# The last down-projection with stationary activations, and a final norm that is finished by half of the rows

## The chip, the cores and the metric

The kernel runs on one core of a Trainium2 chip. The metric is device time in microseconds (us), the median of the runs. Times inside the execution come from one profiled run of the kernel. PE is the matrix engine (TensorE; PEld is its loading of the stationary operand), DVE is VectorE, ACT is ScalarE, POOL is GpSimd, SP is SyncE, which here issues nearly all transfers.

## The reference, cut to what matters

256 tokens of width 2048 go through two layers with a residual stream `h`, and a last RMSNorm. Each layer has a token mixer (a gated MLP in the first, an attention in the second) and a ConvFFN. The end of the program, which the change touches, is the second layer's ConvFFN and the norm behind it:

```python
def rmsnorm(x, g):
    r = lax.rsqrt(jnp.mean(xf * xf, axis=-1, keepdims=True) + EPS)
    return (xf * r).astype(x.dtype) * g

def conv_ffn(xn, w_up, conv_w, conv_b, w_down):      # 2048 -> 2 x 5632 -> 5632 -> 2048
    h = xn @ w_up
    ...                                              # causal conv of width 3, gate, value
    return (jax.nn.silu(gate) * val) @ w_down

h = h + conv_ffn(rmsnorm(h, f_norm[l]), f_w_up[l], f_conv_w[l], f_conv_b[l], f_w_down[l])
...
return rmsnorm(h, final_norm)
```

## The kernel before, in words

**Products.** All weights are float32 and are streamed once from HBM in chunks of 128 x 1024 (512 KB). ACT rounds a chunk to fp32r (`whi`, L84) and DVE makes the remainder (`wlo`, L85); activations are kept as such a pair too (`X1`, `mlp_X2`, `att_X2`, `ffn_H`: columns 0 to 255 the rounded tokens, 256 to 511 the remainders). A product is then three matmuls: rounded by rounded, rounded by remainder, remainder by rounded. One chunk makes 24 matmuls with 256 moving columns each, and each has its own load of a stationary 128 x 128.

**Two roles.** In `feat_block` the weights are stationary and the 256 tokens are moving: the result is feature-major (features on partitions). In `tok_blocks` the activations are stationary, 128 tokens at a time, and the weights are moving: the result is token-major. Stages in the order of the program: `a_in_v` (tok), `a_in_u`, `a_out`, `up0`, `down0` (feat), `b_q` (tok), `kvf_f` (a small one), `kvf_k`, `kvf_v` (tok), `b_g`, `b_out`, `up1`, `down1` (feat). The weights of a `tok` stage lie 32 elements further into their tile than those of a `feat` stage (`FEAT_AT, TOK_AT = 0, 32`, L32).

**Order.** Nothing is scheduled by a tool: `Stream.run` (L88) walks the chunks in order, and for chunk i it issues the load of chunk i+6, the split of chunk i+3, and the products of chunk i; then it steps every pending generator once (`advance`), which is how evictions, norms and transposes are spread over later chunks. Loads wait on SP in this order.

**Wide products.** `between()` (L170) sets `state["wide"]` to `[8, 2]`: of the next chunk 8 matmuls, and of the one after it 2, are issued with 512 moving columns in place of two with 256. It is called where PE does something small between products (sums over tokens, transposes, attention heads), and once in every eleven blocks of `up` (L554).

**The end.** `h` is feature-major, `[128, 16, 256]`. Blocks p = 0 to 6 of `down1` add their result to `h`, square it into `acc` and multiply it with the last gain (`final`, L371). Block 7 goes through `last_tiles` and `last_tile`: its last chunk first finishes one 128-feature tile, then the other. `output` (L389) sums the squares over partitions with matmuls against ones, transposes all of `h` to token-major on PE (32 transposes, L399), computes the factor on ACT and DVE, scales eight 128 x 512 pieces out of PSUM (L420 and L422), and sends 2 MB out with five transfers on SP (L424, L426).

Of the kernel before, what the change touches and what calls it, by code (L numbers as in the profile page):

```python
# [17 lines left out]
P = 128  # L18
# [8 lines left out]
SCALE = 128 ** -0.5  # L27
AHEAD = 3
# [6 lines left out]
C_ANORM, C_KVNORM, C_BNORM, C_FNORM, C_FINAL, C_AVNORM = 0, 16, 32, 48, 80, 96  # L35
C_KNORM, C_QNORM, C_BF = 112, 113, 114
C_CONVW = 115
# [97 lines left out]
def build(ctx, tc, d, out):  # L135
# [8 lines left out]
    col = const.tile([P, C_ALL], F32, name="col")  # L144
    h = const.tile([P, KD, T], F32, name="h")
# [7 lines left out]
    small.tile([P, 56], F32, name="place")  # L153
# [24 lines left out]
    def feat_block(src, x, K, done, tiles=None):  # L178

# [5 lines left out]
        for c in range(n):  # L185
            def mult(hi, lo, c=c):
                if c == 0:
                    box["ps"], box["both"] = tiles[0]() if tiles else main_ps(), False
                ps, xx, wide = box["ps"], x(), wide_next()
                box["both"] |= wide > 0  # L190
                if not tiles:
                    ps = [ps[:, m, :] for m in range(2)]

                def rounded(j, m):
                    nonlocal wide
                    w = hi[:, j * 256 + m * P:j * 256 + (m + 1) * P]
                    kt = 4 * c + j
                    if wide > 0:
                        mm(ps[m], w, xx[:, kt, :], kt == 0, False)
                        wide -= 1  # L200
                    else:
                        for half in range(2):
                            mm(ps[m][:, :T], w, xx[:, kt, half * T:(half + 1) * T], kt == 0 and half == 0, False)

                def remainder(j, m):
                    kt = 4 * c + j
                    mm(ps[m][:, :T], lo[:, j * 256 + m * P:j * 256 + (m + 1) * P], xx[:, kt, :T],
                       False, kt == K - 1)

                if tiles and c == n - 1:  # L210
                    for m in range(2):
                        for j in range(4):
                            rounded(j, m)
                        for j in range(4):
                            remainder(j, m)
                        tiles[1](m, ps[m])
                else:
                    for product in (rounded, remainder):
                        for j in range(4):
                            for m in range(2):  # L220
                                product(j, m)
# [4 lines left out]
    def tok_block(src, x, done):  # L226
        tok_blocks([(src, done)], x)

    def tok_blocks(blocks, x, load=None, prep=None):
# [4 lines left out]
        cuts = [(c, 0, 2) for c in range(8)]  # L234
        if prep:
            cuts[:1] = [(0, 0, 1), (0, 1, 1)]
        for c, j0, nj in cuts:
            if prep and c == 3:
                s.then(at_mult=between)
            for i, ((src, done), box) in enumerate(zip(blocks, boxes)):  # L240
                def mult(hi, lo, c=c, j0=j0, nj=nj, done=done, box=box):
# [4 lines left out]
                    for j in range(nj):  # L246
                        kt = kt0 + j

                        def product(tb, lower, part):
# [3 lines left out]
                            for i in range(0, 512, n):  # L253
                                mm(ps[:, tb, i:i + n], xx[:, kt, at:at + P], part[:, j * 512 + i:j * 512 + i + n],
                                   kt == 0 and i == 0 and part is hi and not lower, kt == KD - 1 and lower == 1)
# [7 lines left out]
                    if kt0 + nj == KD:  # L263
                        s.start(done(ps))
# [86 lines left out]
    def last_tiles():  # L351

        tail["pairs"] = [main_ps() for _ in range(3)]
        tail["banks"] = [misc_ps() for _ in range(2)]
        return tail["pairs"][0][:, 0, :], tail["banks"][0]

    def last_tile(m, ps):

        kt = KD - 2 + m
        if m == 0:  # L360
            tail["sq"] = small.tile([P, 2, T], F32, name="sq", tag="sq", bufs=2)
        nc.vector.tensor_tensor(h[:, kt, :], h[:, kt, :], ps[:, :T], op=OP.add)
        nc.scalar.activation(tail["sq"][:, m, :], h[:, kt, :], AF.Square)
        nc.scalar.activation(h[:, kt, :], h[:, kt, :], AF.Copy, scale=column(C_FINAL + kt))

# [5 lines left out]
    def final(p, gain):  # L371

        def done(ps, both):
            if p == 7:
                output()
                return
            hh = h[:, 2 * p:2 * p + 2, :]
            nc.vector.tensor_tensor(hh, hh, ps[:, :, :T], op=OP.add)
            if both:
                nc.vector.tensor_tensor(hh, hh, ps[:, :, T:], op=OP.add)  # L380
            square_into_acc(p)
            for kt in (2 * p, 2 * p + 1):
                nc.scalar.activation(h[:, kt, :], h[:, kt, :], AF.Copy, scale=column(gain + kt))
            if p == 5:
                nc.scalar.activation(warm, ones, AF.Sqrt)
            yield
        return done

    def output():  # L389

        pairs, banks = tail["pairs"], tail["banks"]
        sums = banks[1]
        place = {(0, 0): pairs[1][:, 0, :], (1, 0): pairs[2][:, 0, :], (0, 1): pairs[1][:, 1, :],
                 (1, 1): pairs[2][:, 1, :], (0, 2): pairs[0][:, 0, :], (1, 2): pairs[0][:, 1, :],
                 (0, 3): banks[0], (1, 3): banks[1]}

        def transposes(tb, quad):
            for j in range(4):
                nc.tensor.transpose(place[tb, quad][:, j * P:(j + 1) * P],  # L399
                                    h[:, 4 * quad + j, tb * P:(tb + 1) * P], ident)  # L400

        sum_tokens(sums, acc, True, False)
        sum_tokens(sums, tail["sq"][:, 0, :], False, False)
        transposes(0, 0)
        sum_tokens(sums, tail["sq"][:, 1, :], False, True)
        t = small.tile([P, 2], F32, name="rs_t", tag="rs_t2", bufs=2)
        v = small.tile([P, 2], F32, name="ts_v", tag="ts_v", bufs=2)
        nc.vector.tensor_scalar(v, sums[:, :2], 1.0 / D, EPS, op0=OP.mult, op1=OP.add)
        nc.scalar.activation(t, v, AF.Sqrt)
        for quad in range(4):  # L410
            for tb in range(2):
                if tb or quad:
                    transposes(tb, quad)
        nc.vector.reciprocal(rcol, t)
        newton(rcol, v, t)
        for quad in range(4):
            o = h[:, 4 * quad:4 * quad + 4, :].rearrange("p a b -> p (a b)").rearrange("p (a b) -> p a b", a=2)
            for tb in range(2):
                if tb == 0:
                    nc.vector.tensor_scalar(o[:, tb, :], place[tb, quad], rcol[:, tb:tb + 1], None, op0=OP.mult)  # L420
                else:
                    nc.scalar.activation(o[:, tb, :], place[tb, quad], AF.Copy, scale=rcol[:, tb:tb + 1])  # L422
                if quad == 0:
                    nc.sync.dma_start(out[quad][:, tb, :], o[:, tb, :])  # L424
            if quad:
                nc.sync.dma_start(out[quad], o)  # L426
# [124 lines left out]
    def ffn(l, done):  # L551
# [4 lines left out]
        for p in range(8):  # L556
            feat_block(d[f"down{l}"][11 * p:11 * p + 11], ffn_h, KF, done(p), (last_tiles, last_tile) if l and p == 7 else None)
# [8 lines left out]
    def blocks_turned(src, n):  # L566


        turned = ph.temp("turned", [P, 512])[:, :n * P].rearrange("p (c h j) -> p c h j", c=4, h=n)
# [318 lines left out]
```

## Time and profile before

| | |
|---|---|
| median of 3 runs | 2194.79 us (2194.67 to 2195.84) |
| the profiled run's own time | 2194.7 us |
| its span, first to last instruction | 2193.0 us |
| PE busy | 2183.9 us of it, 18684 matmuls |
| DVE, ACT busy | 1455.7 us, 1140.6 us |
| DMA | 437.61 MB, mean 200 GB/s |
| granted TensorE clock | 0.999 |

So 1.7 us of the time lie outside the span. Matmuls are pipelined: one matmul of 256 columns is shown as 276 to 282 ns long, and the next starts long before its end, so the pace of PE is the distance between starts (or a count in a stretch of time), and not the length of a row. A row of the timeline merges equal instructions that follow each other; "x16" are 16 of them.

### The profile page before, as it was taken

The page shows a single profiled execution, that of the slowest core. Times are in us where ns is not written, and L with a number is a line of the kernel's source. Part 1 is how long each engine was busy: PE and PEld are TensorE (multiplying, and loading weights), DVE is VectorE, ACT ScalarE, POOL GpSimd, SP SyncE. Part 2 cuts the span into 40 slices and gives each one's busy share as a digit, 9 for nine tenths or more (in the row PEclk, how much of TensorE's full clock was granted, in tenths as well). Part 3 has the DMA queues.
Part 4 walks back from the last instruction along what each step waited for, and adds up shares of the span by engine and source line. Part 5 has one row for each costly group of instructions (what it writes and reads, how often), then busy time and mean ns, then how long its engine had stood idle before and what let it go on. Part 6 is the DMA issues. An engine that isn't in the chain of part 4 may idle for free.

```text
span 2193.0 us, 44738 instructions
## 1 busy us (share of the span) xinstructions
PE 2183.9 (100%) x18684; PEld 2158.3 (98%) x18684; DVE 1455.7 (66%) x2031; ACT 1140.6 (52%) x1517; POOL 19.0 (1%) x41
## 2 busy tenths in 40 slices
PE   9999999999999999999999999999999999999998
PEld 9999999999999999999999999999999999999998
DVE  6676677777777754556786776667777777764443
ACT  5644455555555544444544655455555555544443
POOL 0000000000000000000000100000000000000000
PEclk9999999999999999999999999999999999999999
DMA  8565566666666666666677776556666666666664
GB/s 307 179 188 177 197 197 195 187 202 189 197 194 195 196 184 203 193 196 205 218 226 255 233 227 196 183 197 196 195 195 195 194 193 190 198 197 194 193 194 134
DMA packets 139964, 437.61 MB, mean 200 GB/s; under 512 B 24032, under 2 KB 34672, under 8 KB 139504
## 3 DMA queue, kind: packets, MB, share of 16 engines
q1 hardware_dynamic: 138816, 432.62, 62.4%
q8 instruction: 146, 2.39, 0.5%
q0 software_dynamic: 768, 2.10, 0.4%
q14 instruction: 58, 0.48, 0.1%
q10 hardware_dynamic: 176, 0.02, 0.0%
HBM read 425.22 MB, written 9.45 MB: 198 GB/s over the span
## 4 chain that ended last, share of the span: by engine, by line
PE 99%; DMA 0%; DVE 0%; ACT 0%; ACTq 0%; issue 0%; SPq 0%; DVEq 0%
PE ps L168 97%; PE mp L168 1%; DMA raw<-a_in_v 0%; PE mp L508 0%; PE mp L761 0%; PE mp L760 0%; PE mp L756 0%; PE mp L755 0%; PE mp L754 0%; PE mp L368 0%; DVE h L420 0%; DVE wlo L85 0%; ACT whi L84 0%; ACTq L882 0%; PE mp L308 0%
## 5 line engine op out<-in xcount | busy, mean ns | idle before, releaser
L85 DVE TENSOR_TENSOR wlo<-raw,whi 128x1024 fp32r<-128x1024 f32 (+1 forms) x787 | 954.6, 1219 | 455.2 <-ACT whi L84 447.1
L84 ACT ACTIVATE whi<-raw 128x1024 fp32r<-128x1024 f32 (+1 forms) x787 | 827.3, 1056 | 720.4 <-PE ps L168 655.2
L168 PE MATMUL ps<-X,whi 128*128 128x256 f32 (+1 forms) x6406 | 825.6, 281 | 0.0
L168 PEld LDWEIGHTS ps<-X,whi 128*128 128x128 f32 x6406 | 772.5, 188 | 9.0
L168 PE MATMUL ps<-X,wlo 128*128 128x256 f32 x3328 | 445.4, 276 | 0.0
L168 PEld LDWEIGHTS ps<-X,wlo 128*128 128x128 f32 x3328 | 410.5, 188 | 2.3
L168 PE MATMUL ps<-ffn_H,whi 128*128 128x256 f32 x2728 | 342.7, 276 | 0.0
L168 PEld LDWEIGHTS ps<-ffn_H,whi 128*128 128x128 f32 x2728 | 324.5, 188 | 0.0
L168 PE MATMUL ps<-ffn_H,wlo 128*128 128x256 f32 x1364 | 186.6, 276 | 0.0
L168 PEld LDWEIGHTS ps<-ffn_H,wlo 128*128 128x128 f32 x1364 | 169.9, 188 | 0.0
L542 DVE SCALAR_TENSOR_TENSOR ffn_c<-ffn_a,col,ffn_c 128x255 f32<-128x255 f32 x352 | 162.0, 481 | 6.3
L168 PE MATMUL ps<-whi,att_X 128*128 128x256 f32 (+1 forms) x928 | 164.0, 292 | 0.0
L168 PE MATMUL ps<-whi,X 128*128 128x256 f32 (+1 forms) x989 | 159.1, 281 | 0.2 <-ACT whi L84 0.2
L168 PEld LDWEIGHTS ps<-whi,att_X 128*128 128x128 f32 x928 | 130.5, 188 | 6.2
L168 PEld LDWEIGHTS ps<-whi,X 128*128 128x128 f32 x989 | 133.4, 188 | 2.4 <-ACT whi L84 0.4
L334 DVE TENSOR_TENSOR ffn_a<-ps,rB 128x512 f32<-128x512 f32 x76 | 52.6, 692 | 115.2 <-PE ps L168 115.2
L538 ACT ACTIVATE ffn_c<-ffn_a,col 128x256 f32<-128x256 f32 x176 | 96.3, 594 | 48.8 <-DVE ffn_a L334 48.8
L168 PE MATMUL ps<-wlo,X 128*128 128x256 f32 (+1 forms) x491 | 99.4, 282 | 0.8 <-DVE wlo L85 0.8
L168 PE MATMUL ps<-wlo,att_X 128*128 128x256 f32 (+1 forms) x448 | 100.1, 293 | 0.0
L168 PEld LDWEIGHTS ps<-wlo,X 128*128 128x128 f32 x491 | 74.6, 188 | 1.5 <-DVE wlo L85 1.0
L274 ACT ACTIVATE X<-h,col 128x256 fp32r<-128x256 f32 x64 | 29.1, 501 | 82.4 <-DVE h L340 77.6
L168 PEld LDWEIGHTS ps<-wlo,att_X 128*128 128x128 f32 x448 | 69.9, 188 | 1.9
(157 smaller groups left out, 1133.4 us busy)
## 6 DMA issues: line engine op xcount, KB each, us to landing
raw<-up SPq DMA_DIRECT2D x352, 512.0 KB, 4.0
raw<-down SPq DMA_DIRECT2D x176, 512.0 KB, 3.9
raw<-a_in_u SPq DMA_DIRECT2D x32, 512.0 KB, 4.2
raw<-a_out SPq DMA_DIRECT2D x32, 512.0 KB, 4.3
raw<-b_q SPq DMA_DIRECT2D x32, 512.0 KB, 4.3
raw<-kvf_k SPq DMA_DIRECT2D x32, 512.0 KB, 4.6
raw<-kvf_v SPq DMA_DIRECT2D x32, 512.0 KB, 4.8
raw<-b_g SPq DMA_DIRECT2D x32, 512.0 KB, 4.3
```

The costliest lines, as they stand in the source:

```text
L84: self.nc.scalar.activation(hi[:, :n], raw, AF.Copy)
L85: self.nc.vector.tensor_tensor(lo[:, :n], raw, hi[:, :n].bitcast(F32), op=OP.subtract)
L168: nc.tensor.matmul(o, a, b, start=start, stop=stop, skip_group_check=True)
L274: nc.scalar.activation(dst[:, kt, :T], h[:, kt, :], AF.Copy, scale=g)
L334: nc.vector.tensor_tensor(a, src, rB[:, None, :].to_broadcast([P, 2, T]), op=OP.mult)
L538: nc.scalar.activation(c[:, m, :], a[:, m, :], AF.Identity, scale=w[2], bias=column(C_CONVB + l * 2 * KF + f))
L542: nc.vector.scalar_tensor_tensor(c[:, m, n:], a[:, m, :T - n], w[k], c[:, m, n:], op0=OP.mult, op1=OP.add)
```

## The change

`down1` becomes a `tok` stage. Its 2048 output columns are 3 blocks of 512 (`tok_block`, 22 chunks each), one of 256 (`short_block`, 11 chunks) and a last one of 256 (`last_block`, 11 chunks). All of its matmuls have 256 moving columns. In the last block the products of the second 128 tokens are held back for the last four chunks (`HELD = 4`): first the first 128 tokens are finished for all chunks and `output(0, ...)` is issued, then the 48 held matmuls, then `output(1, ...)`.

The residual stream has to be token-major for this. `residual_by_token`, started in the third block of `up1`, turns `h` in eight pieces: a DVE transpose of 32 x 32 blocks, four transfers to DRAM on SP, and later one transfer back on SP into the same memory. The columns come out in a permuted order, which the host's arrangement of `f_w_down[1]`, of the last gain and of the result follows. The last gain is loaded as a row, broadcast over partitions, on POOL. Sums of squares are taken by ACT as it squares (`accum_out`), so that the end has no sums and no transposes on PE. Two tiles that nothing uses (`spare`, and `place` made larger) keep the other tiles where they were, or move them by 512 bytes a partition in all.

The core of the diff:

```diff
-    small.tile([P, 56], F32, name="place")
+    small.tile([P, 152], F32, name="place")
...
-    def last_tiles():
...
-    def output():
...
+    def residual_by_token():
+        gains = ph.keep("gains", [P, D])
+        nc.gpsimd.dma_start(gains, d["final"].to_broadcast([P, D]))
+        ways = []
+        for tb in range(2):
+            for g in range(4):
+                turned = blocks_turned(h[:, 4 * g:4 * g + 4, tb * P:(tb + 1) * P])
+                yield
+                ways.append(rows_out(f"h{tb}{g}", turned))
+                yield
+        for tb in range(2):
+            for g in range(4):
+                yield
+                rows_in(by_token()[:, tb, g * 512:(g + 1) * 512].rearrange("p (r x) -> p r x", r=4), ways.pop(0))
+
+    def add_block(tb, cols, ps, into):
+        hh = by_token()[:, tb, cols]
+        sq = small.tile([P, 2, T], F32, name="sq", tag="sq", bufs=2).rearrange("p a b -> p (a b)")
+        nc.vector.tensor_tensor(hh, hh, ps, op=OP.add)
+        nc.scalar.activation(sq[:, :ps.shape[1]], hh, AF.Square, accum_out=into)
...
+    def short_products(ps, c, tb, x, K, hi, lo):
+        for j in range(4):
+            kt = 4 * c + j
+            for lower, part in ((0, hi), (0, lo), (1, hi)):
+                at = lower * T + tb * P
+                mm(ps, x()[:, kt, at:at + P], part[:, j * T:(j + 1) * T],
+                   kt == 0 and part is hi and not lower, kt == K - 1 and lower == 1)
+
+    def last_block(src, x, K):
+        n, held, ps = K // 4, [], []
+        for c in range(n):
+            def mult(hi, lo, c=c):
+                if c == 0:
+                    ps.extend(main_ps()[:, 0, :T] for _ in range(2))
+                if c < n - HELD:
+                    for tb in range(2):
+                        short_products(ps[tb], c, tb, x, K, hi, lo)
+                    return
+                held.append((c, hi, lo))
+                short_products(ps[0], c, 0, x, K, hi, lo)
+                if c == n - 1:
+                    output(0, ps[0])
+                    for cc, h2, l2 in held:
+                        short_products(ps[1], cc, 1, x, K, h2, l2)
+                    output(1, ps[1])
+            s.chunk(src[c], mult, TOK_AT)
+
+    def output(tb, ps):
...
+        add_block(tb, last, ps, ss)
+        nc.scalar.activation(t, ss, AF.Sqrt, scale=1.0 / D, bias=v)
+        nc.vector.tensor_tensor(hg, o[:, last], gains[:, last], op=OP.mult)
+        nc.vector.scalar_tensor_tensor(nv, ss, -0.5 / D, nv, op0=OP.mult, op1=OP.add)
+        nc.vector.reciprocal(y, t)
+        nc.vector.tensor_scalar(t, y, y, nv, op0=OP.mult, op1=OP.mult)
+        nc.vector.scalar_tensor_tensor(r, t, 1.5, y, op0=OP.add, op1=OP.mult)
+        nc.scalar.activation(o[:, :512], o[:, :512], AF.Copy, scale=r)
+        nc.scalar.dma_start(out[tb][:, :512], o[:, :512])
+        nc.vector.tensor_scalar(o[:, last], hg, r, None, op0=OP.mult)
+        nc.vector.tensor_scalar(o[:, 1536:1792], o[:, 1536:1792], r, None, op0=OP.mult)
+        nc.sync.dma_start(out[tb][:, 1536:], o[:, 1536:])
+        for blk in (1, 2):
+            cols = slice(blk * 512, (blk + 1) * 512)
+            nc.vector.tensor_scalar(o[:, cols], o[:, cols], r, None, op0=OP.mult)
+            nc.sync.dma_start(out[tb][:, cols], o[:, cols])
...
-    ffn(1, lambda p: final(p, C_FINAL))
+    ffn_up(1)
+    for blk in range(3):
+        tok_block(d["down1"][22 * blk:22 * blk + 22], ffn_h, final(blk), KF)
+    short_block(d["down1s"][:11], ffn_h, KF, final(3))
+    last_block(d["down1s"][11:], ffn_h, KF)
```

How the instructions move, at the two places that the prediction speaks of. The first is PE where `up1` ends and `down1` begins; `X_73` (`X_74` after the change) is `X1`, and "ps<-A,B" has the moving operand A ahead of the stationary B. Before:

```order
L168 MATMUL ps<-X_73,whi 128x256 x16
L168 MATMUL ps<-X_73,wlo 128x256 x8
L168 MATMUL ps<-ffn_H,whi 128x256 x16
L168 MATMUL ps<-ffn_H,wlo 128x256 x8
L168 MATMUL ps<-ffn_H,whi 128x256 x16
L168 MATMUL ps<-ffn_H,wlo 128x256 x8
```

And with the change:

```order
L170 MATMUL ps<-X_74,whi 128x256 x16
L170 MATMUL ps<-X_74,wlo 128x256 x8
L170 MATMUL ps<-whi,ffn_H 128x256 x2
L170 MATMUL ps<-wlo,ffn_H 128x256 x2
L170 MATMUL ps<-whi,ffn_H 128x256 x4
L170 MATMUL ps<-wlo,ffn_H 128x256 x2
L170 MATMUL ps<-whi,ffn_H 128x256 x4
```

The operands change places between two matmuls of 256 columns, and no wide product or other work of PE stands there or anywhere behind it. The second place is the end of the program on DVE. Before:

```order
L362 TENSOR_TENSOR h<-h,ps 128x256
L362 TENSOR_TENSOR h<-h,mp 128x256
L408 TENSOR_SCALAR ts_v<-mp 128x2
L414 RECIPROCAL rcol<-rs_t 128x2
L290 SCALAR_TENSOR_TENSOR rs_t<-rcol 128x2
L291 TENSOR_TENSOR rs_t<-rs_t,ts_v 128x2
L292 SCALAR_TENSOR_TENSOR rcol<-rs_t,rcol 128x2
L420 TENSOR_SCALAR h<-ps,rcol 128x512 x3
L420 TENSOR_SCALAR h<-mp,rcol 128x512
```

With the change these rows stand there for each half of the tokens (here the second half's):

```order
L372 TENSOR_TENSOR h<-h,ps 128x256
L447 TENSOR_TENSOR ffn_hg<-h,ffn_gains 128x256
L448 SCALAR_TENSOR_TENSOR ffn_nv<-ffn_ss,ffn_nv 128x1
L449 RECIPROCAL fin_y<-fin_t 128x1
L450 TENSOR_SCALAR fin_t<-fin_y,ffn_nv 128x1
L451 SCALAR_TENSOR_TENSOR rcol<-fin_t,fin_y 128x1
L454 TENSOR_SCALAR h<-ffn_hg,rcol 128x256
L455 TENSOR_SCALAR h<-h,rcol 128x256
L459 TENSOR_SCALAR h<-h,rcol 128x512 x2
```

The sums that DVE took from PE (L408) are gone, and half as much is scaled behind the last matmul, from SBUF.

More of the change, by code (lines that the diff above doesn't have):

```diff
@@ L187, in mult @@
                 if c == 0:
-                    box["ps"], box["both"] = tiles[0]() if tiles else main_ps(), False
+                    box["ps"], box["both"] = main_ps(), False
                 ps, xx, wide = box["ps"], x(), wide_next()
                 box["both"] |= wide > 0
-                if not tiles:
-                    ps = [ps[:, m, :] for m in range(2)]
                 def rounded(j, m):
@@ L202, in rounded @@
                         for half in range(2):
-                            mm(ps[m][:, :T], w, xx[:, kt, half * T:(half + 1) * T], kt == 0 and half == 0, False)
+                            mm(ps[:, m, :T], w, xx[:, kt, half * T:(half + 1) * T], kt == 0 and half == 0, False)
                 def remainder(j, m):
                     kt = 4 * c + j
-                    mm(ps[m][:, :T], lo[:, j * 256 + m * P:j * 256 + (m + 1) * P], xx[:, kt, :T],
+                    mm(ps[:, m, :T], lo[:, j * 256 + m * P:j * 256 + (m + 1) * P], xx[:, kt, :T],
                        False, kt == K - 1)
[L210 to L221, printed above, removed]
+                for product in (rounded, remainder):
+                    for j in range(4):
+                        for m in range(2):
+                            product(j, m)
                 if c == n - 1:
@@ L254, in product @@
                                 mm(ps[:, tb, i:i + n], xx[:, kt, at:at + P], part[:, j * 512 + i:j * 512 + i + n],
[L255 removed]
+                                   kt == 0 and i == 0 and part is hi and not lower, kt == K - 1 and lower == 1)
                         if nj == 1:
@@ L369, in sum_tokens, with by_token @@
                              start=first and tb == 0, stop=last and tb == 1, skip_group_check=True)
[L371 to L384, printed above, removed]
+    def by_token():
+        return h.rearrange("p a b -> p (a b)").rearrange("p (t f) -> p t f", t=2)
@@ L385, in done @@
                 nc.scalar.activation(warm, ones, AF.Sqrt)
-            yield
         return done
-    def output():
[L391 to L426, printed above, removed]
@@ L555, in ffn @@
                 s.then(at_mult=between)
-        for p in range(8):
-            feat_block(d[f"down{l}"][11 * p:11 * p + 11], ffn_h, KF, done(p), (last_tiles, last_tile) if l and p == 7 else None)
+            if l and i == 2:
+                s.then(at_mult=lambda: s.start(residual_by_token()))
     def att(key):
@@ L809, in build @@
         feat_block(d["a_out"][4 * p:4 * p + 4], mlp_x2, KD, residual(p, C_FNORM))
-    ffn(0, lambda p: residual(p, C_BNORM))
+    ffn_up(0)
+    for p in range(8):
+        feat_block(d["down0"][11 * p:11 * p + 11], ffn_h, KF, residual(p, C_BNORM))
     s.then(at_mult=lambda: s.start(kv_operand()))
```

111 lines of the change are left out of this document (73 added, 38 removed).

## The prediction

> **What bounds the kernel now.** I read the page's first part and the chain of waits, then the end of the timeline, then PE's pace stage by stage.
>
> ```profile
> PE   9999999999999999999999999999999999999998
> PE 99%; DMA 0%; DVE 0%; ACT 0%; ACTq 0%; issue 0%; SPq 0%; DVEq 0%
> ```
>
> PE is never idle, and the chain that ends last is PE for 99%. So two things alone can move the time: the number of matmuls times their pace, and what follows the last matmul. The number does not change: `down1` is 2112 matmuls (88 chunks of 24) in both kernels. The end, first from the chain (start, length):
>
> ```profile
> 2180.25 1.36 PE mp L168 x12
> 2181.61 0.78 PE mp L368 x8
> ```
>
> From the timeline of DVE and ACT, in order of time:
>
> ```profile
> 2181.65 0.42 DVE L362 TENSOR_TENSOR h<-h,mp 128x256 f32<-128x256 f32 x1 [0.94 <-PE mp L168]
> 2182.11 0.42 ACT L363 ACTIVATE sq<-h 128x256 f32<-128x256 f32 x1 [0.40 <-DVE h L362]
> 2183.47 0.20 ACT L409 ACTIVATE rs_t<-ts_v 128x2 f32<-128x2 f32 x1 [0.40 <-DVE ts_v L408]
> 2183.70 0.17 DVE L414 RECIPROCAL rcol<-rs_t 128x2 f32<-128x2 f32 x1 [0.27 <-ACT rs_t L409]
> 2183.90 0.16 DVE L290 SCALAR_TENSOR_TENSOR rs_t<-rcol 128x2 f32<-128x2 f32 x1
> 2184.29 0.16 DVE L292 SCALAR_TENSOR_TENSOR rcol<-rs_t,rcol 128x2 f32<-128x2 f32 x1
> 2184.56 2.07 DVE L420 TENSOR_SCALAR h<-ps,rcol 128x512 f32<-128x512 f32 x3
> ```
>
> And the five output transfers by line, with one microsecond of the table of windows while they run (its last number is GB/s):
>
> ```profile
> L424 SPq DMA_DIRECT2D out<-h x2: 343/384/425, 2185.3 to 2185.7; - x2
> DMA to landing us min/median/max: 2.0/2.2/2.3
> L426 SPq DMA_DIRECT2D out<-h x3: 332/408/412, 2186.3 to 2188.0; - x3
> DMA to landing us min/median/max: 3.1/3.3/4.0
> 2188.00:2189.00 1.00, 0.00 (x0) 0.00 (x0) 0.00 (x0) 0.00 (x0) 0.00 (x0) 1.00 1.01 397
> ```
>
> The last product ends at E = 2181.61 us and the span at 2193.0: 11.4 us. The factor is ready at E + 2.84 (2184.29 + 0.16), the last transfer is issued at 2188.0 and lands 4.0 later, at 2192.0, and 1.0 us of closing work follows. The 2 MB leave at about 400 GB/s. So the end is a chain of small steps and then a transfer.
>
> **PE's pace.** The table of windows gives it: behind the stretch and its length stand PE's busy time and its count, then the same of PEld, DVE, ACT and POOL (where PE was asked for alone, only PE), and the granted clock. Matmuls that each show as 0.28 us touch a stretch W in number N with (W + 0.28) / pace = N.
>
> ```profile
> 1028.00:1068.00 40.00, 40.00 (x355) 1.00 0.77 249
> 2020.00:2100.00 80.00, 80.00 (x708) 1.00 0.60 188
> 97.00:108.00 11.00, 11.00 (x96) 11.00 (x95) 8.79 (x18) 6.14 (x8) 0.00 (x0) 1.00 0.38 125
> 1118.00:1130.00 12.00, 12.00 (x108) 12.00 (x107) 11.66 (x23) 5.18 (x5) 0.00 (x0) 1.00 0.66 186
> ```
>
> The first is `b_q`, with activations stationary as the change wants them: 40.28 / 355 = 113.5 ns. The second is `down1` as it is: 80.28 / 708 = 113.4 ns. Steady, the two roles cost the same. The third is the beginning of `a_in_u`: 11.28 / 96 = 117.5 ns, 4% slower at full clock. The fourth, in `kvf_k`, is fast (113.7) with DVE busy for 11.66 of 12 us, so a busy DVE is not the reason. Where does the slow pace begin and end?
>
> ```profile
> 94.89 0.39 PE L168 MATMUL ps<-whi,X 128*128 128x256 f32 x2
> 95.12 2.04 PE L168 MATMUL ps<-X,whi 128*128 128x256 f32 x16
> ...
> 108.31 1.11 PE L168 MATMUL ps<-X,wlo 128*128 128x256 f32 x8
> 109.25 1.06 PE L508 MATMUL mp<-mlp_wT,mlp_vt 128*128 128x128 f32 x8
> ...
> 995.84 1.07 PE L168 MATMUL ps<-ffn_H,wlo 128*128 128x256 f32 x8
> 996.75 0.40 PE L168 MATMUL ps<-whi,X 128*128 128x256 f32 x2
> ...
> 1002.17 0.40 PE L168 MATMUL ps<-whi,X 128*128 128x256 f32 x2
> 1002.41 0.50 PE L368 MATMUL mp<-ones,acc 128*128 128x1 f32 x4
> ```
>
> Both times it begins at the matmul where the operands change places: from 995.84 to 996.75 stand 8 matmuls at 113.8 ns, from 996.75 to 1002.17 46 (two chunks less two) at 117.8. From 95.12 to 108.31 (112 matmuls) it is 117.8 too. And both times it lasts until PE does something else, the small matmuls at 109.25 and 1002.41 with the wide products that `between` puts behind them. Later the same operands run fast (`b_q` above). It looks like a state that an exchange of roles sets and an interruption clears, not like a property of a role.
>
> **The change part by part.** (1) *Pace.* The exchange from `up1` to the new `down1` is the one at 996.75 again: weights stationary before, activations stationary behind, and the tiles' addresses in the built programs are the same but for 512 bytes in `H`. What cleared the state there is missing: `down1` has no sums, no heads, no wide product. If the state is set and lasts, 2112 matmuls pay 117.8 - 113.4 = 4.4 ns: +9.3 us (4.1 to 4.5 ns by the other quotients: 8.7 to 9.5). If it is not set: 0.
>
> The Trainium skill, page "TensorE: Matmul & The Clock Gate", section "Step-by-step: what each phase is for", says that the two operands come through independent read ports, so that loading the next weights takes nothing from the running matmul. By it the exchange could not matter and this term would be 0; the rows at 95.12 and 996.75 disagree with it in their two stretches.
>
> (2) *The end.* Sums on PE, transposes, four of the eight scalings and 1 MB of transfers leave the stretch behind the last matmul. What stays is priced by the rows above and these (behind the bar: busy us, mean ns):
>
> ```profile
> L483 ACT ACTIVATION_READ_ACCUMULATOR sq<-mlp_vt 128x1 f32 x8 | 1.5, 186 | 0.0
> L633 ACT ACTIVATE att_q<-att_rows,att_gain 128x512 f32<-128x512 f32 x8 | 5.7, 712 | 0.0
> L725 DVE TENSOR_SCALAR att_big<-att_big,att_sm 128x256 f32<-128x256 f32 x16 | 5.6, 348 | 0.0
> L493 DVE TENSOR_SCALAR mlp_vt<-mlp_vt,mlp_rv 128x2048 f32<-128x2048 f32 x2 | 2.5, 1286 | 0.0
> L570 DVE STREAM_TRANSPOSE att_turned<-att_big 128x512 f32<-128x512 f32 x16 | 11.4, 712 | 0.6
> ```
>
> Add to E + 0.46, square to E + 0.92, reading the accumulator (0.19) to E + 1.11, square root to E + 1.33, reciprocal to E + 1.53, two small steps 0.2 apart: the factor at E + 1.93. DVE starts 0.11 later (as 2184.45 to 2184.56), scales 256 columns twice (0.35 each) and 512 twice (0.48 each, an estimate on the line between the rows of 256 and 2048 columns): E + 3.7. ACT's 512 columns (0.71) end before that, at E + 2.8. So the first transfer goes out at E + 2.8, the last at E + 3.8. A transfer of 256 KB took 2.0 to 2.3: E + 6.0; 1 MB at 400 GB/s is 2.6 us behind a start of about 0.9 us (the 2.2 of a 256 KB transfer less its 0.65 of data, rounded down): E + 6.3. I take 6.3, since the four overlap. With 1.0 us of closing work the span ends at E + 7.3 instead of E + 11.4: -4.1 us. Bounds: with the worst landing of the large ones (4.0) E + 8.8 and -2.6; with DVE's pieces at 0.35 each and landings of 2.0, E + 6.5 and -4.9.
>
> The first half must be out of the way: it starts 48 matmuls (5.7 us) earlier, its last scaling ends 3.7 us after that, and its transfers by E + 0.6; the second half wants DVE at E and the queues at E + 2.8. If it were late, at most its 1 MB, 2.6 us, would stand in the way.
>
> (3) *Turning the residual.* 8 transposes of 0.71 us on DVE over 16 chunks of `up1`, 32 small and 8 large transfers on SP, one load on POOL, where nothing stands behind it. What hides it:
>
> ```profile
> 1470.00:1650.00 180.00, 180.00 (x1555) 178.57 (x1554) 132.00 (x186) 101.86 (x138) 0.00 (x0) 1.00 0.63 196
> SPq L578 <- DVE att_turned L570: 3.2, 4, 1.4
> ```
>
> DVE is busy 132 of 180 us in this stage; 5.7 us more in 16 chunks (43.5 us) raise 0.73 to 0.86. On SP the loads of weights stand behind transfers that wait for a transpose: in `b_q`, which does the same exchange eight times, such a wait was 1.4 us at most, and PE's pace there is the 113.5 above. Loads are issued three chunks (8.2 us) ahead of their split. Cost 0; if this cover failed, eight waits of 1.4 us would reach PE: +11 us.
>
> (4) The split of weights, the number and size of the loads, and the evictions' size per chunk stay: 0, under PE as now.
>
> **Sum**, against the profiled span: 2193.0 + 9.3 - 4.1 = 2198.2; with the 1.7 us outside it 2199.9 us. The profiled run (2194.7) lies 0.1 below the median of 2194.79, so the sum can stand beside the median.
>
> **Rivals.** *The fast pace holds* (chance 0.24): the state is not set here, or is left at once. For it: two cases are few, and both lie where a norm changes the work of ACT and DVE as well, which is not so here. Against it: both begin at the very matmul, and keep one pace while the other engines' work goes on changing. Then only the end counts: 2193.0 - 4.1 + 1.7 = 2190.6 us, not slower. By the Trainium skill's rule above this is the case to expect.
>
> *The state is shed on the way* (0.10), for instance where the first block ends, after 528 matmuls (2.3 us): 2192.9 us. For it speaks nothing seen; against it that the stretch at 95.12 passed four edges of chunks, one of them of a block (24 matmuls a chunk, 4 chunks a block), and stayed slow.
>
> *The exchange of the residual starves PE* (0.03): +11 us from (3), 2201.6 with a fast `down1` and 2210.9 with a slow one. Against it speaks `b_q`.
>
> **How the numbers follow.** Slow to the end has 0.63 and gives 2199.9; its own range, 8.7 to 9.5 and -2.6 to -4.9, is 2198.5 to 2201.6. The fast case (2189.8 to 2192.1) holds 0.24, too much to leave out: the range is 2190.0 to 2201.6. What a measurement of this kernel can tell from no change is about 0.2%, 4.4 us: the bounds are 2190.4 and 2199.2. Slower: four fifths of 0.63, and the starved case: 0.53. Faster: half of the fast case: 0.13. The rest, 0.34, is no change that can be told.
>
> **What would show it.** In the profile after, a stretch of 80 us in `down1` would hold about 682 matmuls where 708 were, from the first block on to the last; the last matmul would end about 9 us after 2181.61, and the span 7.3 us behind it. Wrong would be: 708 in 80 us (the first rival); a count that jumps within the stage (the second); idle PE in `up1` (the third); an end of 8.8 us or more; or a slow pace that is there in `up1` already, which would make the exchange of roles the wrong cause.

## The result, and the profile after

| | before | after |
|---|---|---|
| median | 2195.19 us (8 runs, 2194.31 to 2195.9) | 2201.5 us (8 runs, 2200.94 to 2202.2) |
| span of the profiled run | 2193.0 us | 2199.6 us |
| first matmul of `down1` starts | 1942.09 us | 1942.31 us |
| last product of weights ends | 2181.61 us | 2191.21 us |
| from there to the end of the span | 11.4 us | 8.4 us |

The changed kernel takes 1.0029 times the time of the kernel before (95% interval 1.0019 to 1.0038): 0.3% slower, 6.3 us between the medians and 6.6 us between the spans. The products of `down1` take 9.4 us more, the end behind them 3.0 us less, and the stage starts 0.2 us later: 9.4 - 3.0 + 0.2 = 6.6. The 0.2 us were there long before the changed stages: `a_in_u` begins at 95.43 us where it began at 95.12.

The chain that ended last, by engine, is still PE for 99%:

```profile
PE 99%; DMA 0%; DVE 0%; ACT 0%; issue 0%; SPq 0%; DVEq 0%; ACTq 0%
```

The table of windows of the changed kernel, PE alone (stretch, length, busy time and count, granted clock, share of the DMA engines, GB/s). Two stretches lie in `down1`:

```profile
2020.00:2100.00 80.00, 80.00 (x681) 1.00 0.61 189
2100.00:2180.00 80.00, 80.00 (x682) 1.00 0.56 173
```

Where 708 matmuls stood in 80 us there are 681 and 682, at a clock of 1.00 and with PE never idle: 80.28 / 681.5 = 117.8 ns each. The stretch in `up1` in which the residual is turned, all engines:

```profile
1470.00:1650.00 180.00, 180.00 (x1555) 178.54 (x1553) 136.35 (x195) 101.91 (x138) 0.00 (x0) 1.00 0.70 219
```

PE does the same 1555 matmuls as before in it; DVE does 9 instructions and 4.4 us more, and the DMA engines go from 196 to 219 GB/s. PE's timeline at the edge of the stages and at the very end (start, length):

```profile
1941.40 1.07 PE L170 MATMUL ps<-X,wlo 128*128 128x256 f32 x8
1942.31 0.40 PE L170 MATMUL ps<-whi,ffn_H 128*128 128x256 f32 x2
1942.54 0.40 PE L170 MATMUL ps<-wlo,ffn_H 128*128 128x256 f32 x2
...
2190.93 0.28 PE L170 MATMUL ps<-whi,ffn_H 128*128 128x256 f32 x1
```

The eight matmuls of `up1` from 1941.40 to 1942.31 still take 113.8 ns each; the first two of `down1`, 1942.31 to 1942.54, take 115, and the whole stage, first start to last start, (2190.93 - 1942.31) / 2111 = 117.8 ns. What follows the last product, on DVE and in SP's queue:

```profile
2188.16 0.87 DVE L459 TENSOR_SCALAR h<-h,rcol 128x512 f32<-128x512 f32 x2
2191.25 0.42 DVE L372 TENSOR_TENSOR h<-h,ps 128x256 f32<-128x256 f32 x1 [2.22 <-PE ps L170]
2193.08 0.16 DVE L451 SCALAR_TENSOR_TENSOR rcol<-fin_t,fin_y 128x1 f32<-128x1 f32 x1
2193.81 0.88 DVE L459 TENSOR_SCALAR h<-h,rcol 128x512 f32<-128x512 f32 x2
2193.92 0.33 SPq L456 DMA_DIRECT2D out<-h  x1
```

The first half's last scaling ends at 2189.03, the second half's addition starts 0.04 us behind the last product, at 2191.25: the halves overlap as written. The four transfers of the second half go out between 2193.9 and 2194.8. Their landing, from the view of line 460 (first and last issue, then the time to landing):

```profile
L460 SPq DMA_DIRECT2D out<-h x4: 378/614/862, 2188.7 to 2194.8; - x4
DMA to landing us min/median/max: 3.1/3.2/3.4
```

And one of the two microseconds with most traffic, from the windows (the next one has 385 GB/s):

```profile
2195.00:2196.00 1.00, 0.00 (x0) 0.00 (x0) 0.00 (x0) 0.00 (x0) 0.00 (x0) 0.50 1.02 383
```

The last transfer lands by 2194.8 + 3.4 = 2198.2, and 1.4 us later the span ends.

### The profile page after: what moved, and what is told of

Same layout as the page of the kernel before. It is cut to its first block, busy times and chain, and to the rows that moved or that the text cites. A ratio compares the mean times of both kernels' runs of the same rounds, so it can differ in the third digit from the quotient of the medians.

```text
span 2199.6 us, 44730 instructions
## 1 busy us (share of the span) xinstructions
PE 2188.8 (100%) x18640; PEld 2163.4 (98%) x18640; DVE 1461.9 (66%) x2047; ACT 1134.6 (52%) x1511; POOL 19.2 (1%) x42
## 4 chain that ended last, share of the span: by engine, by line
PE 99%; DMA 0%; DVE 0%; ACT 0%; issue 0%; SPq 0%; DVEq 0%; ACTq 0%
PE ps L170 98%; DMA raw<-a_in_v 0%; PE mp L542 0%; PE mp L803 0%; PE mp L797 0%; PE mp L798 0%; PE mp L802 0%; PE mp L796 0%; DVE wlo L86 0%; ACT whi L85 0%; PE mp L344 0%; PE mp L299 0%; DVE h L459 0%; ACT sq L373 0%; DVE h L372 0%
## 5 line engine op out<-in xcount | busy, mean ns | idle before, releaser
L170 PE MATMUL ps<-whi,ffn_H 128*128 128x256 f32 x1408 | 229.9, 281 | 0.0
L170 PEld LDWEIGHTS ps<-whi,ffn_H 128*128 128x128 f32 x1408 | 197.2, 189 | 0.0
L170 PE MATMUL ps<-ffn_H,whi 128*128 128x256 f32 x1408 | 173.9, 276 | 0.0
L170 PEld LDWEIGHTS ps<-ffn_H,whi 128*128 128x128 f32 x1408 | 166.1, 188 | 0.0
L170 PE MATMUL ps<-wlo,ffn_H 128*128 128x256 f32 x704 | 154.8, 281 | 0.0
L325 DVE TENSOR_TENSOR ffn_a<-ps,rB 128x512 f32<-128x512 f32 x76 | 52.5, 691 | 113.4 <-PE ps L170 113.4
L170 PEld LDWEIGHTS ps<-wlo,ffn_H 128*128 128x128 f32 x704 | 114.6, 189 | 0.0
L170 PE MATMUL ps<-ffn_H,wlo 128*128 128x256 f32 x704 | 94.2, 276 | 0.0
```

Source lines behind the costliest of these rows:

```text
L170: nc.tensor.matmul(o, a, b, start=start, stop=stop, skip_group_check=True)
L325: nc.vector.tensor_tensor(a, src, rB[:, None, :].to_broadcast([P, 2, T]), op=OP.mult)
```

## The experiments

The theory on trial at first is the prediction's: exchanging the operands' roles sets a longer pace that lasts, and an interruption clears it. A rival is that token-major products with these tiles are simply slow in `down1`. Later a third view came up: that the places of the tiles decide.

### Does a wide product at the exchange bring the pace back?

One line is added to the changed kernel, so that the first two chunks of `down1` have 8 and 2 products of 512 columns in place of pairs of 256:

```diff
     ffn_up(1)
+    s.then(at_mult=between)
     for blk in range(3):
         tok_block(d["down1"][22 * blk:22 * blk + 22], ffn_h, final(blk), KF)
```

> The changed kernel with ten wide products behind the exchange of roles (8 in the first chunk of down1, 2 in the second). My theory, that the exchange sets a slow state which wide products clear: down1 runs at 113.4 ns a matmul, about 708 in 80 us, and the time falls from 2201.5 by 2112 x 4.4 ns = 9.4 us to about 2192 us, 3 us below the kernel before. Rival, that token-major products of down1 are slow in themselves (its H, its 44 rows of K): 117.8 ns and 2201.5 us as without them.

Measured: 2191.89 us (11 runs, 2191.23 to 2192.79) beside 2194.92 for the kernel before: 0.9985 times its time (0.9976 to 0.9994). PE's timeline of this kernel behind the eight wide products of the first chunk:

```profile
1944.91 0.64 PE L170 MATMUL ps<-whi,ffn_H 128*128 128x256 f32 x4
1945.38 0.40 PE L170 MATMUL ps<-wlo,ffn_H 128*128 128x256 f32 x2
1945.62 0.63 PE L170 MATMUL ps<-whi,ffn_H 128*128 128x256 f32 x3
...
1946.79 0.39 PE L170 MATMUL ps<-wlo,ffn_H 128*128 128x256 f32 x2
...
1948.15 0.39 PE L170 MATMUL ps<-wlo,ffn_H 128*128 128x256 f32 x2
```

And its windows:

```profile
2020.00:2100.00 80.00, 80.00 (x708) 1.00 0.64 194
```

Behind the eight, 1944.91 to 1945.62, six matmuls still take 118 ns each. Behind the two of the second chunk, 1946.79 to 1948.15, twelve take 113.3, and so it stays (708 in 80 us are 113.4). The same products, tiles and addresses are therefore not slow in themselves. The whole loss of 9.4 us hangs on this line: 2201.5 - 2191.9 = 9.6.

### Can it be cleared in the middle of the stage?

```diff
     for blk in range(3):
+        if blk == 1:
+            s.then(at_mult=between)
         tok_block(d["down1"][22 * blk:22 * blk + 22], ffn_h, final(blk), KF)
```

> The same ten wide products, but only where the second block of down1 begins, 528 matmuls later. My theory: the first block at 117.8 ns, everything behind it at 113.4 ns, so 528 x 4.4 ns = 2.3 us of the 9.4 stay: about 2194.4 us. Rival (slow in itself): 117.8 ns throughout, 2201.5 us. If the state needed the exchange itself to be disturbed: also 2201.5 us.

Measured in one run: 2193.59 us. The first stretch is in the first block, the second behind the wide products:

```profile
1950.00:2000.00 50.00, 50.00 (x426) 1.00 0.59 186
2020.00:2100.00 80.00, 80.00 (x708) 1.00 0.63 194
```

50.28 / 426 = 118.0 ns, then 113.4. So it is a state: it lasted for 528 matmuls while loads, splits and evictions went on, and ended with the wide products. Here the eight of the first chunk did it already, as the timeline behind them shows:

```profile
2005.64 0.62 PE L170 MATMUL ps<-whi,ffn_H 128*128 128x256 f32 x4
2006.10 0.39 PE L170 MATMUL ps<-wlo,ffn_H 128*128 128x256 f32 x2
2006.33 0.61 PE L170 MATMUL ps<-whi,ffn_H 128*128 128x256 f32 x3
```

2005.64 to 2006.33 are six matmuls at 115 ns on average, before the next wide product comes (in the trace's starts the first lasts 119 ns, the others 113 to 114). Eight wide products as the first of the stage did not end the state, eight inside it did.

### Does any other work of PE clear it?

In place of the wide products, two small transposes stand at the exchange. Their result is not used.

```diff
+    def small_work():
+        mp = misc_ps()
+        for tb in range(2):
+            nc.tensor.transpose(mp[:, tb * P:(tb + 1) * P], rcol[:, tb:tb + 1].to_broadcast([P, P]), ident)
+
+    s.then(at_mult=small_work)
```

> The changed kernel with two small transposes on PE at the exchange of roles, and no wide product. If any interruption clears or forestalls the state: 113.4 ns in down1 and about 2192 us. If the wide products are what clears it: 117.8 ns and about 2201.7 us. The trace of before speaks a little for the second, since at 112.02 us eight matmuls behind small work and eight wide products were still slow.

Measured in one run: 2202.04 us. PE's timeline at the edge:

```profile
1942.86 0.38 PE L873 MATMUL mp<-ident,rcol 128*128 128x128 f32 x2
1942.99 0.48 PE L170 MATMUL ps<-whi,ffn_H 128*128 128x256 f32 x2
```

A stretch of the stage from its windows:

```profile
2020.00:2100.00 80.00, 80.00 (x682) 1.00 0.61 186
```

The small work stands between the stages, and the pace is slow all the same. Not any interruption clears the state. In the two places of the kernel before from which the prediction read that, small matmuls and wide products came together; the small ones get no credit. In that kernel itself the eight matmuls behind the small work at 109.25 us and eight wide products (from 112.02 us) still run at 118 ns.

How few wide products are enough? Here none in the first chunk and two in the second:

```diff
+    s.then(at_mult=lambda: state.update(wide=[0, 2]))
```

> The changed kernel with only two wide products, in the second chunk of down1 (24 matmuls behind the exchange of roles). In the run with ten, the eight of the first chunk left the state slow and the pace turned right behind the two of the second. If two are enough: 113.3 ns from there on and 2192.0 us. If all ten are needed: 117.8 ns and 2201.5 us.

Measured in one run: 2192.65 us. PE's timeline in the second chunk:

```profile
1946.01 0.40 PE L170 MATMUL ps<-wlo,ffn_H 128*128 128x512 f32 x1
```

A stretch of the stage from its windows:

```profile
1950.00:2000.00 50.00, 50.00 (x444) 1.00 0.65 200
```

50.28 / 444 = 113.2 ns: two inside the stage are enough.

### Is the longer pace bound to the token-major form?

Now the kernel before, with feature-major products in `down1`. Ahead of them 24 matmuls with exchanged roles are put (activations stationary, weights moving); they are additional and their result is not used.

```diff
...
+                if c == 0 and turn:
+                    mp = misc_ps()
+                    for i in range(24):
+                        mm(mp[:, :T], xx[:, i // 4, :P], hi[:, 32 + 256 * (i % 2):288 + 256 * (i % 2)], True, True)
...
```

> The kernel before, feature-major to the end, with 24 matmuls of exchanged roles (activations stationary, 256 weights moving, result unused) put between up1 and down1: the roles change there and back, and nothing else of the change is in it. My theory, each exchange sets the slow state: the 24 and the 2112 behind them at 117.8 ns, 2195.2 + 2.8 + 9.4 = 2207.4 us. If an exchange turns the state over, so that two cancel: only the 24 are added, 2198.0 us. Rival, that down1's token-major products are slow in themselves: 2198.0 us too, with the 24 alone at 117.8 ns.

Measured in one run: 2206.58 us. PE's timeline at the beginning of the stage:

```profile
1941.75 2.99 PE L168 MATMUL mp<-whi,ffn_H 128*128 128x256 f32 x24
1944.58 2.05 PE L168 MATMUL ps<-ffn_H,whi 128*128 128x256 f32 x16
```

A stretch of the stage from its windows:

```profile
2020.00:2100.00 80.00, 80.00 (x682) 1.00 0.58 185
```

The additional matmuls take 2.8 us (1941.75 to 1944.58), and the 2112 feature-major ones behind them, which ran at 113.4 ns before, all run at 117.8: 2.8 + 2112 * 4.4 ns = 12.1 us, measured 2206.58 - 2194.92 = 11.7. The state is not bound to one of the two forms.

### Does the place of the operands matter? A step of 128 bytes

The weights of `tok` stages lie 128 bytes further into their tile than those of `feat` stages. In the kernel before, `down1` gets the place of the `tok` stages (`at` is `TOK_AT` for `down1` alone):

```diff
...
-            s.chunk(src[c], mult, FEAT_AT)
+            s.chunk(src[c], mult, at)
...
```

In the kernel of the first experiment (wide products at the exchange) `down1` gets the place of the `feat` stages:

```diff
...
-            s.chunk(src[c], mult, TOK_AT)
+            s.chunk(src[c], mult, FEAT_AT)
...
```

> The kernel before, feature-major to the end and with no exchange of roles, but the weights of down1 lie 32 elements (128 bytes) further into their tiles, where token-major stages have them. If the exchange of roles is what sets the slow state: 113.3 ns and 2195 us as before. If the state comes from where the moving and the stationary operand lie to each other in SBUF (in all stages of both kernels the start of the moving operand less that of the stationary one is 192 bytes, modulo 256; here it is 64): slower than 113.3 ns from the first matmul of down1 on; at 117.8 ns 2204.5 us.

> The changed kernel with the ten wide products behind the exchange, but the weights of down1 at the offset of feature-major stages (0), so that moving less stationary is 64 bytes modulo 256, in place of 192. If only the exchange matters: 113.3 ns behind the wide products, 2192 us. If the places of the operands set which paces there are: slower in the steady state although the wide products stand there; at 117.8 ns 2201.5 us.

Measured in one run each: 2194.89 us and 2191.65 us. One stretch of the first of them, then one of the second:

```profile
2020.00:2100.00 80.00, 80.00 (x708) 1.00 0.62 189
```

```profile
2020.00:2100.00 80.00, 80.00 (x708) 1.00 0.65 196
```

Neither changes anything. Taken alone this speaks against a part for the places; the next run shows that the step was badly chosen.

### A step of 64 bytes

In the built programs the weights' tile `whi` starts at byte 160 of a 256-byte line, its `tok` part (128 bytes on) at 32, `X1` at 96, and `ffn_H` (like `mlp_X2` and `att_X2`, which use the same memory) at 96. The pieces that the matmuls of these stages take begin whole multiples of 128 bytes behind these places. The changed kernel, without any wide product at the exchange, gets the last three moved by 64 bytes, to 160, and the weights of `down1` with them, so that within `down1` the two operands stand to each other as they did.

```diff
-    small.tile([P, 152], F32, name="place")
+    small.tile([P, 168], F32, name="place")
...
-            s.chunk(src[c], mult, TOK_AT)
+            s.chunk(src[c], mult, 48)
...
```

> The changed kernel without wide products in down1, with the pool of H (and of the mixers' operands) 64 bytes further on, and the weights of down1 64 bytes further into their tiles. So down1's own operands lie to each other as before, but at the exchange the stationary H lies 64 bytes, modulo 256, from the moving X1, where both lay at the same place. In down0, a_out and b_out moving less stationary becomes 0 in place of 192, in kvf_k and kvf_v 128, with no exchange changed. If the exchange of roles as such sets the slow state: down1 at 117.8 ns, the other stages at 113.3 ns, 2201.5 us. If the coincidence of places at the exchange sets it: down1 at 113.3 ns and 2192 us. If the places decide the steady pace at this step: down0 (2112 matmuls), a_out or kvf_k leave 113.3 ns; with down0 at 117.8, 9.4 us more.

Measured in one run: 2222.42 us, 20.9 us slower than the changed kernel (the second edit is in `down1` alone). Windows of this kernel, in `a_out`, `down0`, `kvf_k`, `b_out` and `down1`:

```profile
200.00:240.00 40.00, 40.00 (x336) 1.00 0.57 184
800.00:900.00 100.00, 100.00 (x836) 1.00 0.60 189
1169.00:1199.00 30.00, 30.00 (x255) 1.00 0.78 255
1405.00:1485.00 80.00, 80.00 (x669) 1.00 0.56 181
2000.00:2080.00 80.00, 80.00 (x709) 1.00 0.62 192
```

And the first two of these stages in the kernel before:

```profile
200.00:240.00 40.00, 40.00 (x355) 1.00 0.55 183
800.00:900.00 100.00, 100.00 (x885) 1.00 0.63 194
```

`down1` runs at 80.28 / 709 = 113.2 ns from its first block on, with the roles exchanged and nothing there to clear a state. So an exchange of roles as such does not set it, and this part of the theory falls. In its place `a_out` and `down0`, which exchange nothing, are slower than any stage so far: 40.28 / 336 = 119.9 and 100.28 / 836 = 120.0 ns against 113.5 and 113.3. So are `b_out`, 80.28 / 669 = 120.0 ns, and `kvf_k`, 30.28 / 255 = 118.7 ns; `kvf_k` ran at 113.7 before. From their starts in the trace `a_out` is 4.9 us longer than in the changed kernel, `down0` 14.1, `kvf_k` and `kvf_v` together 6.0, `b_out` 5.4, and `down1` is 9.4 us shorter. The timeline at the edge of `down0` and `b_q` in this kernel:

```profile
1015.26 1.12 PE L170 MATMUL ps<-ffn_H,wlo 128*128 128x256 f32 x8
1016.22 0.39 PE L170 MATMUL ps<-whi,X 128*128 128x256 f32 x2
1016.45 0.39 PE L170 MATMUL ps<-wlo,X 128*128 128x256 f32 x2
1016.68 0.62 PE L170 MATMUL ps<-whi,X 128*128 128x256 f32 x4
1017.13 0.39 PE L170 MATMUL ps<-wlo,X 128*128 128x256 f32 x2
```

Eight matmuls of `down0` take 0.96 us (120 ns each), and from 1016.45 on `b_q` runs at (1017.13 - 1016.45) / 6 = 113 ns, where the kernel before ran at 117.8 behind the same edge. From `a_out` to `up0` it shows this, behind a stage at 120 ns:

```profile
284.78 1.07 PE L170 MATMUL ps<-X,wlo 128*128 128x256 f32 x8
285.69 1.98 PE L170 MATMUL ps<-X,whi 128*128 128x256 f32 x16
287.50 1.07 PE L170 MATMUL ps<-X,wlo 128*128 128x256 f32 x8
```

`up0` begins at 282.95, and the 24 matmuls from 284.78 to 287.50 already take 113.3 ns each. With the places of the operands beside each other, modulo 128 bytes:

| | moving operand at | stationary operand at | apart, modulo 128 | pace |
|---|---|---|---|---|
| within `down0`, before | `ffn_H` 96 | `whi` 160 | 64 | 113.3 ns |
| within `down0`, moved by 64 bytes | `ffn_H` 160 | `whi` 160 | 0 | 120.0 ns |
| within `a_out` and `b_out`, moved by 64 bytes | `mlp_X2`, `att_X2` 160 | `whi` 160 | 0 | 119.9, 120.0 ns |
| within `kvf_k`, before | `whi` 32 | `att_X2` 96 | 64 | 113.7 ns |
| within `kvf_k`, moved by 64 bytes | `whi` 32 | `att_X2` 160 | 0 | 118.7 ns |
| within `down1`, weights 128 bytes on (kernel before) | `ffn_H` 96 | `whi` 32 | 64 | 113.4 ns |
| edge `down0` to `b_q`, before (last moving, next stationary) | `ffn_H` 96 | `X1` 96 | 0 | 117.8 ns behind it |
| edge `up1` to `down1`, after | `X1` 96 | `ffn_H` 96 | 0 | 117.8 ns behind it |
| edge `up1` to `down1`, before | `X1` 96 | `whi` 160 | 64 | 113.4 ns behind it |
| edge `up1` to the 24 additional matmuls, kernel before | `X1` 96 | `ffn_H` 96 | 0 | 117.8 ns in them |
| edge from these 24 to `down1`, kernel before | `whi` 32 | `whi` 160 | 0 | 117.8 ns behind it |
| edge `a_in_v` to `a_in_u`, before | `whi` 32 | `whi` 160 | 0 | 117.8 ns behind it |
| edge `down0` to `b_q`, moved by 64 bytes | `ffn_H` 160 | `X1` 96 | 64 | 113 ns behind it |
| edge `up1` to `down1`, moved by 64 bytes | `X1` 96 | `ffn_H` 160 | 64 | 113.2 ns behind it |
| edges `a_out` to `up0` and `b_out` to `up1`, moved by 64 bytes | `mlp_X2`, `att_X2` 160 | `whi` 160 | 0 | 113.3 ns behind them |

Within the stages all rows fit one reading: PE is slowed, to 118.7 to 120.0 ns, where the operand that it streams and the stationary operand that it loads meanwhile stand at the same place modulo 128 bytes. A period of 256 would not do: in `kvf_k` the two stand 128 bytes apart and it is slow.

At the edges the same reading, that one coincidence leaves the state of 117.8, holds for eight rows and not for the last. Five of the eight have the coincidence, between stages whose own operands stand 64 bytes apart, and PE was slow behind it; three lack it, and PE was fast. Behind `a_out` and `b_out`, which ran at 120, it left nothing after a few matmuls. Nor is a coincidence needed. In the kernel before, PE is fast up to the sums over tokens at 61.61 us (302 matmuls from 27 to 61 us, 113.5 ns); behind them and eight wide products, it is slow, with no exchange of roles and with operands 64 bytes apart where the sums begin (`whi` 32, `acc` 96) and 32 where they end (`ones` 0, `X1` 96):

```profile
63.91 0.63 PE L168 MATMUL ps<-whi,X 128*128 128x256 f32 x4
64.39 0.40 PE L168 MATMUL ps<-wlo,X 128*128 128x256 f32 x2
64.62 0.40 PE L168 MATMUL ps<-whi,X 128*128 128x256 f32 x2
```

From 63.91 to 64.62 stand six matmuls at 118 ns. The run with the two transposes does not fit simply either: the last operand streamed ahead of `down1` there is `ident`, 32 bytes from `ffn_H` modulo 128 (`X1` and `rcol`, one edge earlier, do coincide). So that moving these tiles took the slow state away from `down1` is shown, by one run that moved three tiles and the weights at once; what in general sets the state at an edge, and why it then lasts for 2112 matmuls, stays open.

### What is the overlap of the halves worth?

The kernel of the first experiment, with one held chunk in place of four:

```diff
-HELD = 4
+HELD = 1
```

> The changed kernel with the ten wide products, and the second half's products held for the last chunk alone (12 matmuls, 1.4 us) in place of four (48, 5.4 us). My theory of the end: the first half's work on DVE, 3.5 us from its last product, then stands in the way of the second half's for 2.1 us, and the transfers follow each other: the stretch from the last product to the end grows from 8.4 to 10.5 us and the time from 2191.9 to 2194.0 us. If the transfers alone set the end, 1 MB more stands there: +2.6 us, 2194.5. If the overlap of the halves brings nothing: 2191.9.

Measured: 2193.78 us (10 runs, 2193.47 to 2194.56); 0.9995 times the time of the kernel before (0.9985 to 1.0005), against 0.9985 with four. PE's last product in this kernel:

```profile
2181.43 0.28 PE L170 MATMUL ps<-whi,ffn_H 128*128 128x256 f32 x1
```

DVE's additions of the two halves:

```profile
2180.38 0.42 DVE L372 TENSOR_TENSOR h<-h,ps 128x256 f32<-128x256 f32 x1 [7.20 <-PE ps L170]
2183.73 0.42 DVE L372 TENSOR_TENSOR h<-h,ps 128x256 f32<-128x256 f32 x1
```

The second half's addition starts 2.0 us behind the last product (2183.73 - 2181.71), without idle time before it: it stands in DVE's queue behind the first half's steps. The end is 2192.1 - 2181.71 = 10.4 us instead of 8.4. So four held chunks instead of one are worth 2.0 us of the end's gain of 3.0, and in the changed kernel their cover has 2.2 us to spare (2191.25 - 2189.03).

### Wide products at the other slow edges

`a_in_u` and `b_q` begin slow wherever the tiles have their old places. The first experiment, with one more item at each:

```diff
+    s.then(at_mult=between)
     for p in range(8):
         feat_block(d["a_in_u"][4 * p:4 * p + 4], lambda: X1, KD, u_done(p))
...
     s.then(at_mult=lambda: s.start(kv_operand()))
+    s.then(at_mult=between)
     for blk in range(4):
         tok_block(d["b_q"][8 * blk:8 * blk + 8], lambda: X1, head_norm("q", blk))
```

> The changed kernel with ten wide products behind each of three exchanges of roles: into down1 as in the first experiment, and into a_in_u and b_q, where 119 and 46 matmuls are slow now. My theory: both stretches go to 113.3 ns behind the first chunks, 0.3 to 0.7 us less than with the one, about 2191.3 us, and 3.5 to 4 us below the kernel before. If those stretches are slow for another reason (the work of ACT and DVE there): 2191.9 us, and their pace stays.

Measured: 2193.15 us (11 runs, 2192.29 to 2193.8), 1.3 us slower than the first experiment where 0.3 to 0.7 less was expected. The view of waits between 994 and 1003 us, the beginning of `b_q` (total, times, longest):

```profile
PEld ps L170 <- DVE wlo L86: 1.1, 1, 1.1
PE ps L170 <- DVE wlo L86: 0.8, 1, 0.8
```

PE waits for the split of weights (0.4 us more for ACT's part, `whi`). Such an item takes a place in the stream: the split runs three items ahead, so it was one chunk less ahead. In the next kernel the call at `b_q` goes into an item that is there anyway (the one ahead of `a_in_u` stays):

```diff
-    s.then(at_mult=lambda: s.start(kv_operand()))
+    s.then(at_mult=lambda: (between(), s.start(kv_operand())))
```

> The first experiment's kernel with wide products behind the exchanges into a_in_u and b_q too, but the one into b_q is set in an item of the stream that is there already, so that the splits of weights are not one chunk later there. If it was the extra item that made PE wait 1.9 us in b_q: no wait, a_in_u 0.45 us shorter and b_q 0.1 us, in all 2191.4 us against 2191.9 with the one. If the wide products made it wait: 2193 us again.

Measured: 2191.2 us (11 runs, 2190.74 to 2191.8) beside 2194.95: 0.9982 times the time of the kernel before (0.9973 to 0.9991), and no wait of PE in that stretch. In `a_in_u` the products of 256 columns behind the wide ones are fast: 80 from 99.2 to 108 us, (8.8 + 0.28) / 80 = 113.5 ns. This is the fastest kernel of the study; its lead of 0.7 us on the first experiment is less than the intervals can tell.

## Why the prediction was right, and where it was not

**The forecast.** 2199.9 us and slower was said as the likeliest, 2201.5 measured, within the likeliest case's own range of 2198.5 to 2201.6, at its upper edge. Of the 1.6 us between them the end is 1.1; the rest is the 0.1 of the pace, the 0.2 by which `down1` starts later, and 2.0 us outside the span where 1.7 were taken over.

**Step 1, the pace: right in place and size.** 9.4 us against 9.3; 681 and 682 matmuls in 80 us against about 682; from the first block to the last. The forecast that nothing in `down1` would clear the state held too. The Trainium skill, page "TensorE: Matmul & The Clock Gate", section "Step-by-step: what each phase is for", says that loading the next stationary operand takes no read bandwidth from the running matmul, by which this term was 0. The runs do not bear it out: the same 2112 matmuls took 113.4 or 117.8 ns, and those of `down0` 113.3 or 120.0 after a move of one operand by 64 bytes.

**Step 1, the cause: too broad in one word and wrong in another.** "An interruption clears it" came from two places where small matmuls and wide products stand together; the small ones alone cleared nothing (2202.04 us), two wide ones did. "An exchange of roles sets it" fell with the tiles moved by 64 bytes, where the same exchange left 113.2 ns. What the prediction noted in passing, that the addresses were the same but for 512 bytes, was what made its analogy with the edge at 996.75 hold: 512 is a multiple of 128. To carry over a measured edge with the same tiles was sound; that a shift of 512 bytes did no harm was luck, since nothing seen until then told which shifts matter. In the run with the moved tiles, where `place` is 64 bytes longer, the same sentence gives a wrong pace at this edge. Its reading of the trace was narrow too: "both times" counts two exchanges, while the same pace stands at 63.91 us with no exchange ahead of it.

**Step 2, the end: right in kind, 1.1 us too good.** 3.0 us saved against 4.1, within the bounds of 2.6 to 4.9. With E the end of the last product, 2191.21: the factor was ready at E + 2.03 (2193.24) against 1.93, DVE's last scaling at E + 3.5 (2194.69) against 3.7, the last transfer out at E + 3.6 against 3.8. So the steps of computing fit. The transfers do not: the last landed by E + 7.0 against 6.3, and the closing work was 1.4 us against 1.0. The mis-sized term is the landing, and in it the start of 0.9 us: the difference that the prediction names for it, 2.2 less 0.65, is 1.55 and not 0.9. With 1.55 the sum E + 2.8 + 1.55 + 2.6 is E + 6.95, close to the E + 7.0 measured. The rate is a small part of it, 383 and 385 GB/s in the microseconds 2195 to 2197 where 400 was assumed. That the closing work is no constant was not thought of; why it grew is not shown.

**Step 3, the residual: right.** PE is never idle in `up1`, and `down1` begins 0.2 us later than before, a delay that was there at `a_in_u` already (0.3 us).

**The rivals.** The fast pace (2190.6 us) is what the changed kernel with wide products shows (2191.9), so its sum was a good one for a case that needed one line more. A state shed on the way did not occur by itself; made by hand at the second block it gave 2193.59 us where the rival had 2192.9. Starved PE did not occur in `up1`, but the mechanism is real: an item too many in front of `b_q` cost about 2 us (2193.15 us with it, 2191.2 without).

## What to carry to other kernels

Read the pace of matmuls as a distance between starts, stage by stage and on both sides of every edge: a PE that is 99% busy at full clock can still lose 4 to 6%, and no row of idle time shows it. Where tiles or stages are rearranged, write down where the moving and the stationary operand start, modulo 128 bytes, within the stage above all and across its edge; if an edge makes the stage behind it slow, try two products of 512 columns in the stage's second chunk before undoing the change. And put such a call into an item of the stream that exists, since an item of its own takes one chunk from the lookahead.

## What the runs showed of the hardware that was not expected

- The pace of the same matmuls (256 moving columns, a load of the stationary operand for each) was 113.3, 117.8 or, within stages whose operands coincide modulo 128 bytes, 118.7 to 120.0 ns at a granted clock of 1.00, by where the operands lay and by what ran before.
- The state of 117.8 ns lasted for 2112 matmuls, was there behind two small transposes too, and ended with two products of 512 columns inside the stage; eight as the stage's first products did not end it. Why stays open.
- A move by 128 bytes changed nothing in two kernels; a move by 64 bytes slowed `a_out`, `down0`, `kvf_k`, `kvf_v` and `b_out`, and cost 20.9 us in all, although `down1` itself gained.
- Transfers of 256 KB landed in 2.0 to 2.3 us as the first two of the kernel before (line 424), and in 3.1 to 3.4 us as the last two of each half after the change (line 460). The closing work behind the last landing was 1.4 us where it had been 1.0.
